# Half-size loads for the last w_out blocks, an earlier fetch of the second token tile, and new places in memory

## The chip, the cores and the metric

The kernel runs on one core of a Trainium2 chip. The metric is the device time of one execution in microseconds (us). The engines of the core are named as the profile names them: PE (TensorE; PEld is its weight load), DVE (VectorE), ACT (ScalarE), POOL (GpSimd) and SP (SyncE, which here issues nearly all transfers).

## The reference

One layer of a diffusion backbone on 2048 latent tokens of width 1024, with 256 context tokens, in fp32:

```python
hc = modulate(rmsnorm(xc, norm_mix[l]), csh1, csc1)
logf_f, k_f, logf_b, k_b, vc = hgrn2_gates(hc @ w_in[l][:, :3 * w], lb_f, lb_b, first)
hf_c = advance_state(h0, k_f, vc, jnp.cumsum(logf_f, axis=2))
hb_c = advance_state(h0, flip_t(k_b), flip_t(vc), jnp.cumsum(flip_t(logf_b), axis=2))
h = modulate(rmsnorm(x, norm_mix[l]), sh1, sc1)
o, _, _ = token_mixers(h @ w_in[l], lb_f, lb_b, first, hf_c, hb_c, *mix_args)
x = x + g1 * (o @ w_out[l])
h2 = modulate(rmsnorm(x, norm_ffn[l]), sh2, sc2)
x = x + g2 * conv_ffn(h2, w_up[l], conv_w[l], conv_b[l], w_down[l], rows)
return rmsnorm(x, norm_final)
```

`token_mixers` is a gated linear recurrence in both directions (4 heads) beside a spatial gating unit (4 heads); their outputs, 8 blocks of 128 channels, are the 8 row blocks that `w_out` (1024x1024) multiplies. `conv_ffn` is a gated MLP of width 2816 with a depthwise 3x3 convolution: up-projection, convolution and GELU, product, down-projection.

## The kernel before

Matrix products keep fp32 accuracy by splitting each operand into a high part (a copy on ACT, line 133, into the matmul's own float type) and a low part (the difference, line 134, on VectorE or GpSimd). Three matmuls stand for one product: high by high, high by low, low by high (`mm3`, line 136). All are recorded at line 65.

The work runs in four stages, one after the other on TensorE.

1. Input projection (`pj` tiles). The columns of `w_in` are taken block by block over halves of 1024 tokens, with the recurrence, the gating and preparations of later weights as generators in two queues (`hg_q`, `bg_q`), stepped between matmuls. One generator, `w_out_ops` (line 981), multiplies each 128x512 piece of `w_out` by the gate `g1`, splits it, and stores both parts to DRAM (`wo_d`).
2. Output projection (`dn` tiles out of `wo` and `o`). Sixteen token tiles of 128 rows; each takes 2 halves of 512 columns, 8 row blocks k, 3 matmuls: 48 matmuls. The operand `o` of a token tile is fetched from DRAM (`fetch_o`, line 1313) and split (`split_o`, line 1319). Tile t's operand is split before tile t-1's matmuls are written; even tiles use one buffer, odd tiles another. Between the matmuls stand the transposes and casts of the second norm (`second_norm`).
3. Up-projection (`ux`, `uz` tiles), by a 7-product scheme on 2x2 blocks, with operands `Ah`, `Al` from `a_tiles` (line 1198); the convolution runs beside it on VectorE in PSUM tiles also named `dn`.
4. Down-projection (`dn` tiles of a second pool), again 7 products, each over 11 pairs of row blocks: 77 steps n, each 8 token tiles of 3 matmuls. `prepare(n + 2)` calls `cast` (line 1541), which splits the activations into `mhl` and the weights into `thl`. After 11 steps the eight PSUM banks are emptied by `evict` (line 1789). The last product's rows are normed in `odd_sum`, `root` (line 1719) and `odd_out`.

Around the border between stages 1 and 2: during the last head, `wo_early` (line 918) loads the first three row blocks of `wo` into places that come free. Four banks before the end of stage 1, `open_wo` (line 1126) closes a pool and queues `load`, which fetches token tile 0's operand and then row blocks 3 to 7, in two column halves of 512 KB each (line 1144). The operand of tile 1 is fetched after the stage has ended, by `fetch_o(1)`.

A scheduler orders each engine's instructions by its own estimate of when they are ready. `pin` keeps an instruction behind the one written before it on its engine. Pools opened one after the other take over memory; a tile in memory that was another tile's waits for that tile's last readers.

Of the kernel before, what the change touches and what calls it, by code (L numbers as in the profile page):

```python
# [9 lines left out]
F32 = mybir.dt.float32  # L10
# [8 lines left out]
P = 128  # L19
D = 1024  # L20
# [11 lines left out]
EPS = 1e-6  # L32
LV = [1, 2, 4, 8, 16, 32, 64]
AL = 512

# [46 lines left out]
def tile_trunk(ctx, tc, x, c, cx, c_ctx, w_ada, b_ada, norm_mix, norm_ffn, w_in, hg_norm, sgu_g, sgu_b,  # L84
# [12 lines left out]
    dr = ctx.enter_context(tc.tile_pool(name="dr", bufs=1, space=DRAM))  # L97
    ident = cst.tile([P, P], F32, name="ident")
    make_identity(nc, ident)
    ones = cst.tile([P, P], F32, name="ones")  # L100
    G.memset(ones, 1.0)
    ones_r = cst.tile([P, P], F32R, name="ones_r")
    nc.gpsimd.tensor_copy(ones_r, ones)
    vec = cst.tile([P, 50], F32, name="vec")
    taps = cst.tile([P, 9 * NF], F32, name="taps")
    mhalf = cst.tile([P, 8], F32, name="mhalf")
# [24 lines left out]
    def split(hi, lo, raw, eng=None, keep=lambda i: i):  # L131

        keep(S.copy(hi, raw))  # L133
        (eng or G).tensor_sub(lo, raw, hi.bitcast(F32))  # L134
# [56 lines left out]
    with es1:  # L191
# [790 lines left out]
        def w_out_ops():  # L982

            for n in range(2):
                cl = slice(n * 512, n * 512 + 512)
                g = pm.tile([P, 512], F32, tag="acc", name="g1")
                ld(g, g_d[0:1, cl].broadcast_to([P, 512]))
                for k in range(NK):
                    raw = raw_tile().rearrange("p (a c) -> p a c", a=2)
                    hi, w = raw[:, 0, :], raw[:, 1, :]  # L990
                    ld(w, w_out[k * P:(k + 1) * P, cl])
                    yield 8.0
                    V.tensor_mul(w, w, g)
                    split(hi.bitcast(F32R), w.bitcast(F32R), w, V)
                    st(wo_d[:, k, :, cl], raw)
                    yield 1.5

        def w_down_ops():
# [128 lines left out]
        def open_wo():  # L1127
            hg_q.drain()
            gates_done()
            bg_q.drain()  # L1130
            esh.close()
            pw = esw.enter_context(tc.tile_pool(name="pw", bufs=1, side="right", reuse_waits="tile"))
            first_o.append(lambda: pw.tile([P, 2, NK, P], F32R, tag="o", name="o", align_bytes=AL))
            early = len(wo)

            def load():
                raw = raw_tile().rearrange("p (k c) -> p k c", c=P)
                ld(raw, oT_d[0][:, :, 0:P])
                for k in range(early, NK):
                    wo.append(pw.tile([P, 2, D], F32R, name=f"wo{k}", align_bytes=AL))  # L1140
                for n in range(2):
                    sl = slice(n * 512, n * 512 + 512)
                    for k in range(early, NK):
                        ld(wo[k][:, :, sl].bitcast(F32), wo_d[:, k, :, sl])
                yield 17.0
                o = first_o[0]()
                split(o[:, 0], o[:, 1], raw, V, pin)
                first_o.append(o)
                yield 0.0
            bg_q.add(load())  # L1150
# [9 lines left out]
        run_banks(seq)  # L1160
        bg_q.drain()
        hg_q.flush()

# [11 lines left out]
    xah = pb.tile([P, NR, 4, 512], F32R, tag="xah", name="xah", align_bytes=AL)  # L1177
    xal = pb.tile([P, NR - 1, 4, 512], F32R, tag="xal", name="xal", align_bytes=AL)

    turn = [0]  # L1180

    def xbank():
        return ps2.tile([P, 512], F32, tag="ux", name="ux", bufs=2)

    def zbank():
        return ps2.tile([P, 512], F32, tag="uz", name="uz", bufs=2)

    def ubank():
        turn[0] += 1
# [2 lines left out]
    def dbank():  # L1192
        return ps2.tile([P, 2, 512], F32, tag="dn", name="dn", bufs=2)

    def a_tiles():
        return tuple(px.tile([P, 4, P], F32R, tag=w, name=w, bufs=4, align_bytes=AL) for w in ("Ah", "Al"))

    def v_tile():
        return px.tile([P, TH + GW], F32, tag="cv", name="cv", bufs=3)

    def c_tile():
        return px.tile([P, NK, P], F32R, tag="fl", name="fl", bufs=2, align_bytes=AL)

    def raw_tile2(j):
        return px.tile([P, 4, 2 * P], F32, tag=f"raw{j}", name="raw")
# [2 lines left out]
    class Unit:  # L1208
# [15 lines left out]
        def prep(self, i):  # L1224

            a11, a21 = self.raw[0][:, :, :P], self.raw[0][:, :, P:]
            a12, a22 = (self.raw[1][:, :, :P], self.raw[1][:, :, P:]) if i else (None, None)
            self.A[i] = a_tiles()
            hi, lo = self.A[i]

            if i == 1:
                self.s2 = (c_tile()[:, :4, :].bitcast(F32) if self.slots[0] == 1 else
                           px.tile([P, 4, P], F32, tag="s1", name="s2"))
            split(hi, lo, (a11, a12, self.s2, a11, a21, a12, a22)[i])
            if i == 0:
                G.tensor_sub(a21, a11, a21)
            elif i == 1:
                pin(G.tensor_sub(self.s2, a22, a21))
            elif i == 2:
                G.tensor_add(a11, self.s2, a11)  # L1240
            elif i == 3:
                G.tensor_sub(a12, a12, self.s2)
# [30 lines left out]
    with tc.tile_pool(name="po", bufs=1, reuse_waits="tile") as po:  # L1273
        def second_norm(hh, g0, xs, ss, bank_, first, step):

            r = rstd(px, ss, 2, 1.0 / D)
            for i in range(2):
                scaled.append(V.tensor_scalar(out=xs[i], in0=xs[i], scalar1=r[:, i:i + 1], scalar2=None, op0=ALU.mult))
            yield first
            cl = slice(g0 // 2 * P, g0 // 2 * P + P)  # L1280
            for k in range(4):
                pt = bank_()
                for kk in range(2):
                    for i in range(2):
                        o = kk * 256 + i * P
                        T.transpose(pt[:, o:o + P], xs[i][:, (k + 4 * kk) * P:(k + 4 * kk + 1) * P], ident)
                yf = c_tile()
                fl = yf.bitcast(F32)
                for kk, dims in ((0, [[7 * P, 2], [1, P]]), (1, [[4 * P, 2], [1, P]])):
                    kq = k + 4 * kk  # L1290
                    pin(S.activation(view(fl, kk * P, dims),
                                     pt[:, kk * 256:kk * 256 + 256].rearrange("p (i c) -> p i c", c=P),
                                     AF.Identity, bias=s2[:, kq:kq + 1], scale=a2[:, kq:kq + 1]))
                pin(V.tensor_sub(fl[:, 3:5, :], view(fl, 7 * P, [[-2 * P, 2], [1, P]]), view(fl, 0, [[7 * P, 2], [1, P]])))
                V.tensor_sub(fl[:, 2, :], fl[:, 5, :], fl[:, 3, :])
                V.tensor_sub(fl[:, 6, :], fl[:, 1, :], fl[:, 2, :])
                hi = px.tile([P, 7, P], F32R, tag="yst", name="yst", bufs=2, align_bytes=AL)
                a = b = 0
                if hh == 0:
                    a, b = NR, NR - 1  # L1300
                    S.copy(xah[:, :, k, cl], fl[:, :a, :])
                    V.tensor_sub(xal[:, :, k, cl], fl[:, :b, :], xah[:, :b, k, cl].bitcast(F32))
                    V.tensor_sub(yf[:, b:a, :], fl[:, b:a, :], xah[:, b:a, k, cl].bitcast(F32))
                split(hi[:, a:, :], yf[:, a:7, :], fl[:, a:7, :], V)
                st(yd[hh][:, 0, a:, k, cl], hi[:, a:, :].bitcast(F32))
                st(yd[hh][:, 1, b:, k, cl], fl[:, b:7, :])
                yield step
# [9 lines left out]
            return raw  # L1317

        def split_o(t, raw):
            o = po.tile([P, 2, NK, P], F32R, tag="o", name="o", align_bytes=AL) if t % 2 else first_o[0]()  # L1320
            split(o[:, 0], o[:, 1], raw, V, pin)
            return o

# [2 lines left out]
            ld(xt.rearrange("p a b -> p (a b)"), x[t * P:(t + 1) * P, :])  # L1326
            return xt.rearrange("p a b -> p (a b)")

        raw_o = {1: fetch_o(1)}
        xts = {0: fetch_x(0)}  # L1330
        ops = {0: first_o[1]}
        xs = []
        for t, (hh, g) in enumerate(tiles):
            if g % 2 == 0:
# [205 lines left out]

    def cast(n, a, b, at, bt):

        split(*at, a, V)
        split(*bt, b, V)
        ops[n] = *at, *bt

    def down(pd, n, i, first, last):
# [18 lines left out]
    for n, (u, i) in enumerate(prods):  # L1566
# [18 lines left out]
        if n == 11:  # L1585
            bg_q.drain()
        if n == 12:
            edges = px.tile([P, 7, P], F32R, tag="yst", name="edges", bufs=2, align_bytes=AL).bitcast(F32)
            edges = edges[:, :4, :].rearrange("p f (w c) -> p f w c", w=2)
        with tc.issue_after(scaled[-1].ins) if n < 8 else nullcontext():  # L1590
            after(u, i, p)
# [37 lines left out]
    pd_ = ctx.enter_context(tc.tile_pool(name="pd", bufs=1, reuse_waits="tile"))  # L1629
    sT = pb.tile([P, NR * 4 * 512], F32, tag="xah", name="sT", align_bytes=AL)  # L1630
    sS = pd_.tile([P, NJ, TH], F32, tag="sS", name="sS", align_bytes=AL)
    thl = pd_.tile([P, 3, 2, 512], F32R, name="thl", align_bytes=AL)
    odd = [pd_.tile([P, 2, 512], F32, name=f"odd{i}") for i in range(NCH)]
    even = [pd_.tile([P, 2, 512], F32, name=f"even{i}") for i in range(NCH)]
    nf = pd_.tile([P, D], F32, name="nf")
    nw = [0]
# [82 lines left out]
    def root(ss, plus=D * EPS):  # L1719

        a, r = (pd_.tile([P, 1], F32, tag=t, name=t, bufs=4) for t in ("ra", "rr"))
        G.tensor_scalar(out=a, in0=ss, scalar1=plus, scalar2=None, op0=ALU.add)  # L1722
        G.tensor_tensor(out=r, in0=a, in1=mhalf[:, :1], op=ALU.pow)  # L1723
        return r

# [63 lines left out]
    def evict(q, i, pd):  # L1789
        o, e = odd[i], even[i]  # L1790
        if q in (0, 2):
            S.copy(o[:, q // 2, :], pd)
        elif q in (1, 5):
            V.tensor_add(e[:, q // 5, :], pd, e[:, q // 5, :])
        elif q in (3, 4):
            V.tensor_add(o[:, 0, :], pd, o[:, 0, :])
        sums_behind(q, i)
# [65 lines left out]
```

## Time and profile before

| What | Value |
|---|---|
| Time of three runs, median (lowest to highest) | 2437.95 us (2434.5 to 2441.58) |
| The profiled execution's own time | 2440.39 us |
| Its span (first to last instruction) | 2438.6 us |
| TensorE busy | 2402.0 us (99%) |
| VectorE, ScalarE, GpSimd busy | 1656.9, 1043.2, 867.8 us |
| Mean granted TensorE clock | 0.996 |
| Moved by DMA | 396.43 MB, mean 163 GB/s |

A busy share is an average over stages. Matmuls are pipelined, so the mean duration of one (389 ns) is longer than the step from one start to the next. An idle time in brackets stands before the instruction on its line, with the one that ended it.

### The profile page before, as it was taken

The numbers are of one execution on the slowest core, as the hardware profiler recorded it, in microseconds if no ns is written. First come the engines' busy times: TensorE is split into PE (matmuls) and PEld (weight loads), VectorE is DVE, ScalarE is ACT, GpSimd is POOL, SyncE is SP. The second block draws the span as 40 slices with busy tenths as digits, with TensorE's granted clock in tenths as the row PEclk, the third lists the DMA queues.
The fourth block names the chain that finished last, engine by engine and source line by source line (L and its number), as shares of the span: only waits on it lengthen the run. The fifth ranks groups of instructions, "written<-read, shape, count | busy, mean of one in ns | idle before, by whom it ended". The sixth has DMA issues, their size and how long they took to land.

```text
span 2438.6 us, 32286 instructions
## 1 busy us (share of the span) xinstructions
PE 2402.0 (99%) x11711; PEld 1995.0 (82%) x11711; DVE 1656.9 (68%) x2253; ACT 1043.2 (43%) x1802; POOL 867.8 (36%) x788
## 2 busy tenths in 40 slices
PE   8999999999999999999999999999999999999998
PEld 5887887888888888788888888888888887888887
DVE  5757795765786785465596666639866772776875
ACT  3654344444444443354554444434445442332343
POOL 0021110210121122000688778787888870000002
PEclk9999999999999999999999999999999999999999
DMA  8365445463355234668922322562222238934755
GB/s 302 117 206 169 148 143 168 153 234 111 114 195 173 88 103 160 223 208 264 303 80 90 96 81 91 179 235 97 86 94 85 88 112 336 324 121 147 229 152 198
DMA packets 305581, 396.43 MB, mean 163 GB/s; under 512 B 32633, under 2 KB 215681, under 8 KB 302349
## 3 DMA queue, kind: packets, MB, share of 16 engines
q1 hardware_dynamic: 302132, 393.61, 48.6%
q8 instruction: 92, 1.51, 0.3%
q10 hardware_dynamic: 3289, 0.76, 0.1%
q14 instruction: 68, 0.56, 0.1%
HBM read 285.18 MB, written 109.13 MB: 162 GB/s over the span
## 4 chain that ended last, share of the span: by engine, by line
PE 54%; issue 2%; DMA 1%; DVE 1%; POOL 1%; ACT 1%; SPq 0%; POOLq 0%; ACTq 0%; DVEq 0%
PE dn L65 20%; PE ux L65 19%; PE uz L65 14%; PE pj L65 0%; POOL ra L1722 0%; DMA raw<-in_x_dram 0%; POOL rr L1723 0%; PE ux L69 0%; DMA raw<-in_w_up_dram 0%; DMA yf<-yd 0%; PE uz L69 0%; DVE dn L1433 0%; DMA yd<-fl 0%; POOL Al L134 0%; DVE cv L1357 0%
## 5 line engine op out<-in xcount | busy, mean ns | idle before, releaser
L1433 DVE SCALAR_TENSOR_TENSOR dn<-gp,taps,dn 128x1024 f32<-128x1024 f32 x352 | 448.2, 1284 | 97.5 <-ACT dn L1430 93.1
L65 PE MATMUL dn<-thl,mhl 128*128 128x512 f32 x1680 | 381.5, 389 | 1.2 <-ACT thl L133 1.2
L65 PEld LDWEIGHTS dn<-thl,mhl 128*128 128x128 f32 x1680 | 315.0, 188 | 67.7 <-ACT thl L133 2.1
L134 POOL TENSOR_TENSOR Al<-raw,Ah 128x512 fp32r<-128x512 f32 x264 | 341.7, 1311 | 65.8 <-ACT Ah L133 41.5
L65 PE MATMUL pj<-xh,whi 128*128 128x512 f32 x896 | 362.3, 405 | 0.3 <-ACT whi L133 0.3
L65 PE MATMUL pj<-xh,wlo 128*128 128x512 f32 x896 | 351.1, 392 | 1.2 <-DVE wlo L134 1.2
L65 PE MATMUL pj<-xl,whi 128*128 128x512 f32 x896 | 351.7, 393 | 0.0
L133 ACT CAST Ah<-raw 128x512 fp32r<-128x512 f32 x264 | 162.9, 620 | 238.9 <-PE ux L65 133.1
L65 PE MATMUL ux<-xah,Ah 128*128 128x512 f32 x528 | 205.7, 390 | 0.3 <-ACT keep L1497 0.3
L65 PEld LDWEIGHTS pj<-xh,wlo 128*128 128x128 f32 x896 | 168.3, 188 | 37.5 <-DVE wlo L134 2.1
L65 PEld LDWEIGHTS pj<-xh,whi 128*128 128x128 f32 x896 | 168.7, 188 | 34.2 <-issue 3.5
L65 PEld LDWEIGHTS pj<-xl,whi 128*128 128x128 f32 x896 | 168.9, 189 | 30.0 <-DVE xl L253 0.2
L65 PE MATMUL dn<-wo,o 128*128 128x512 f32 x768 | 184.4, 396 | 2.6 <-ACT o L133 2.1
L65 PE MATMUL uz<-yf,Ah 128*128 128x512 f32 x704 | 174.0, 389 | 0.0
L65 PEld LDWEIGHTS dn<-wo,o 128*128 128x128 f32 x768 | 143.0, 189 | 32.8 <-ACT o L133 2.5
L591 POOL TENSOR_TENSOR K<-K,tot 128x512 f32<-128x512 f32 x40 | 62.9, 1572 | 299.9 <-DVE tot L521 154.6
L65 PE MATMUL ux<-yf,Ah 128*128 128x512 f32 x528 | 155.4, 389 | 0.0
L65 PEld LDWEIGHTS uz<-yf,Ah 128*128 128x128 f32 x704 | 132.1, 188 | 27.4
L65 PE MATMUL ux<-xah,Al 128*128 128x512 f32 x528 | 141.8, 390 | 1.0 <-POOL Al L134 0.9
L65 PE MATMUL ux<-xal,Ah 128*128 128x512 f32 x352 | 137.0, 389 | 0.0
L1722 POOL TENSOR_SCALAR ra<-ss 128x1 f32<-128x1 f32 x8 | 5.3, 662 | 360.4 <-ACT jk L1714 360.4
L134 DVE TENSOR_TENSOR wlo<-raw,whi 128x1024 fp32r<-128x1024 f32 x68 | 84.1, 1236 | 68.3 <-ACT whi L133 67.3
(341 smaller groups left out, 4452.7 us busy)
## 6 DMA issues: line engine op xcount, KB each, us to landing
raw<-in_w_up_dram SPq DMA_DIRECT2D x88, 512.0 KB, 3.6
mr<-m SPq DMA_DIRECT2D x85, 512.0 KB, 5.5
raw<-in_w_in_dram SPq DMA_DIRECT2D x68, 512.0 KB, 4.0
sT<-wd SPq DMA_DIRECT2D x88, 256.0 KB, 5.8
raw<-in_w_ada_dram SPq DMA_DIRECT2D x32, 512.0 KB, 4.6
yf<-yd SPq DMA_DIRECT2D x14, 1024.0 KB, 10.4
m<-cv SPq DMA_DIRECT2D x22, 544.0 KB, 2.7
raw<-in_w_down_dram SPq DMA_DIRECT2D x22, 512.0 KB, 4.0
```

The lines of the kernel that those rows point to most:

```text
L65: return self.engine.matmul(out, lhsT, rhs, **kw)
L133: keep(S.copy(hi, raw))
L134: (eng or G).tensor_sub(lo, raw, hi.bitcast(F32))
L591: e.tensor_mul(view(K2, row * W + o, src), view(K, o, src), view(tot, t0, [[4, n], [ts, 2], [0, B]]))
L1433: V.scalar_tensor_tensor(out=cr, in0=gt[:, t // 3:t // 3 + RH, t % 3:t % 3 + GW], scalar=taps[:, t * NF + f:t * NF + f + 1], in1=cr, op0=A ...
L1722: G.tensor_scalar(out=a, in0=ss, scalar1=plus, scalar2=None, op0=ALU.add)
```

## The change

It has these parts:

- Row blocks k = 5, 6, 7 of `w_out` (`LATE`) are no longer split in stage 1: the product with the gate alone is stored, and at the border only that is loaded (256 KB for a half instead of 512 KB) and split there, behind the last bank of stage 1, on ACT and VectorE, the low part in the loaded data's place.
- The operand of token tile 1 is fetched into a tile of its own, `raw1`, directly behind the row blocks, instead of by `fetch_o(1)` after the stage.
- In stage 4, `thl` is placed behind the first five `odd` tiles; the copies of `cast` (steps 3 to 65) and of `evict` are pinned in the written order on ACT.
- `root` adds a tensor where it added a scalar operand read from memory.
- Places: `ones` shares the memory of `ones_r`; the late `wo` tiles share one tag; `Ah` and `Al` share one tag of eight buffers; some tiles no longer ask for a multiple of 512 bytes, and `s2` is made 80 elements longer; the PSUM tags of stages 2 and 3 are laid out in a fixed order, `uz` as two tags of one buffer each.

```diff
+LATE = (5, 6, 7)
...
-    ones = cst.tile([P, P], F32, name="ones")
-    G.memset(ones, 1.0)
     ones_r = cst.tile([P, P], F32R, name="ones_r")
-    nc.gpsimd.tensor_copy(ones_r, ones)
+    nc.gpsimd.tensor_scalar(out=ones_r, in0=ident, scalar1=0.0, scalar2=1.0, op0=ALU.mult, op1=ALU.add)
+    ones = ones_r.bitcast(F32)
...
                     V.tensor_mul(w, w, g)
-                    split(hi.bitcast(F32R), w.bitcast(F32R), w, V)
-                    st(wo_d[:, k, :, cl], raw)
+                    if k in LATE:
+                        st(wo_d[:, k, 0, cl], w)
+                    else:
+                        split(hi.bitcast(F32R), w.bitcast(F32R), w, V)
+                        st(wo_d[:, k, :, cl], raw)
...
                 for k in range(early, NK):
-                    wo.append(pw.tile([P, 2, D], F32R, name=f"wo{k}", align_bytes=AL))
+                    wo.append(pw.tile([P, 2, D], F32R, tag="wo", name="wo", bufs=NK - early, align_bytes=AL))
                 for n in range(2):
                     sl = slice(n * 512, n * 512 + 512)
                     for k in range(early, NK):
-                        ld(wo[k][:, :, sl].bitcast(F32), wo_d[:, k, :, sl])
+                        if k in LATE:
+                            ld(wo[k][:, 1, sl].bitcast(F32), wo_d[:, k, 0, sl])
+                        else:
+                            ld(wo[k][:, :, sl].bitcast(F32), wo_d[:, k, :, sl])
+                raw1 = pw.tile([P, NK, P], F32, name="raw1")
+                ld(raw1, oT_d[0][:, :, P:2 * P])
+                first_o.append(raw1)
                 yield 17.0
...
         bg_q.drain()
         hg_q.flush()
+        for n in range(2):
+            sl = slice(n * 512, n * 512 + 512)
+            for k in LATE:
+                t = wo[k][:, :, sl]
+                split(t[:, 0], t[:, 1], t[:, 1].bitcast(F32), V, pin)
...
     def zbank():
-        return ps2.tile([P, 512], F32, tag="uz", name="uz", bufs=2)
+        turn[1] += 1
+        return ps2.tile([P, 512], F32, tag=f"uz{turn[1] % 2}", name="uz")
...
+    for first in (xbank, zbank, dbank, zbank):
+        first()
...
-        return tuple(px.tile([P, 4, P], F32R, tag=w, name=w, bufs=4, align_bytes=AL) for w in ("Ah", "Al"))
+        return tuple(px.tile([P, 4, P], F32R, tag="A", name=w, bufs=8, align_bytes=AL) for w in ("Ah", "Al"))
...
-            o = po.tile([P, 2, NK, P], F32R, tag="o", name="o", align_bytes=AL) if t % 2 else first_o[0]()
+            o = po.tile([P, 2, NK, P], F32R, tag="o", name="o") if t % 2 else first_o[0]()
...
-        raw_o = {1: fetch_o(1)}
+        raw_o = {1: first_o[1]}
...
-        split(*at, a, V)
-        split(*bt, b, V)
+        keep = pin if 3 <= n < 6 * NJ else lambda i: i
+        split(*at, a, V, keep)
+        split(*bt, b, V, keep)
...
+    odd = [pd_.tile([P, 2, 512], F32, name=f"odd{i}") for i in range(5)]
     thl = pd_.tile([P, 3, 2, 512], F32R, name="thl", align_bytes=AL)
-    odd = [pd_.tile([P, 2, 512], F32, name=f"odd{i}") for i in range(NCH)]
+    odd += [pd_.tile([P, 2, 512], F32, name=f"odd{i}") for i in range(5, NCH)]
...
-        G.tensor_scalar(out=a, in0=ss, scalar1=plus, scalar2=None, op0=ALU.add)
+        if isinstance(plus, float):
+            G.tensor_scalar(out=a, in0=ss, scalar1=plus, scalar2=None, op0=ALU.add)
+        else:
+            G.tensor_add(a, ss, plus)
...
         if q in (0, 2):
-            S.copy(o[:, q // 2, :], pd)
+            pin(S.copy(o[:, q // 2, :], pd))
```

More of the change, by code (lines that the diff above doesn't have):

```diff
@@ L1201, in c_tile @@
     def c_tile():
-        return px.tile([P, NK, P], F32R, tag="fl", name="fl", bufs=2, align_bytes=AL)
+        return px.tile([P, NK, P], F32R, tag="fl", name="fl", bufs=2)
     def raw_tile2(j):
@@ L1232, in prep @@
                 self.s2 = (c_tile()[:, :4, :].bitcast(F32) if self.slots[0] == 1 else
[L1233 removed]
+                           px.tile([P, 4 * P + 80], F32, tag="s1", name="s2")[:, :4 * P].rearrange("p (k c) -> p k c", k=4))
             split(hi, lo, (a11, a12, self.s2, a11, a21, a12, a22)[i])
@@ L1296, in second_norm @@
                 V.tensor_sub(fl[:, 6, :], fl[:, 1, :], fl[:, 2, :])
-                hi = px.tile([P, 7, P], F32R, tag="yst", name="yst", bufs=2, align_bytes=AL)
+                hi = px.tile([P, 7, P], F32R, tag="yst", name="yst", bufs=2)
                 a = b = 0
@@ L1587, in tile_trunk @@
         if n == 12:
-            edges = px.tile([P, 7, P], F32R, tag="yst", name="edges", bufs=2, align_bytes=AL).bitcast(F32)
+            edges = px.tile([P, 7, P], F32R, tag="yst", name="edges", bufs=2).bitcast(F32)
             edges = edges[:, :4, :].rearrange("p f (w c) -> p f w c", w=2)
```

4 lines of the change are left out of this document (2 added, 2 removed).

## The prediction

> **What bounds the kernel now.** I read the head of the page first, then TensorE's waits, then the order of time around each wait. The page says which engine sets the end:
>
> ```profile
> span 2438.6 us, 32286 instructions
> PE 2402.0 (99%) x11711; PEld 1995.0 (82%) x11711; DVE 1656.9 (68%) x2253; ACT 1043.2 (43%) x1802; POOL 867.8 (36%) x788
> 1237.76 5.44 PE ux L65 x24
> ```
>
> TensorE is busy in all but 37 us of the span. The third line, from the chain of work that ended last, gives its pace: 24 matmuls of 128x512 in 5.44 us, 0.2267 us from start to start. The change removes no matmul, so only stalls, clock and the ends of the program can give anything. TensorE's waits (engine and line, waited for whom: us, times, longest) name the candidates:
>
> ```profile
> PE pj L65 <- DMA wa<-in_w_ada_dram: 3.3, 4, 1.5
> PE sc L65 <- DVE kl L800: 2.7, 2, 2.0
> PE dn L65 <- ACT o L133: 2.1, 1, 2.1
> PE dn L65 <- ACT thl L133: 1.2, 2, 0.8
> PE dn L65 <- DVE o L134: 0.5, 1, 0.5
> ```
>
> The third and fifth are the border between the input projection and the output projection, the fourth is the down stage; the change works on both. The first two lie in the projection, where it only takes side work away.
>
> **The border.** The order of time there (start, duration, engine, line; in brackets the idle time before and who ended it):
>
> ```profile
> 962.94 0.39 SPq L1144 DMA_DIRECT2D wo<-wo_d  x1
> 963.72 0.59 SPq L1138 DMA_DIRECT2D raw<-oT  x1
> 964.35 7.24 SPq L1144 DMA_DIRECT2D wo<-wo_d  x9
> 969.95 1.05 ACT L133 CAST o<-raw 128x1024 fp32r<-128x1024 f32 x1 [2.81 <-DMA raw<-oT]
> 972.96 0.60 ACT L690 ACTIVATE gu<-pj 128x512 f32<-128x512 f32 x1 [1.96 <-PE pj L65]
> 973.43 2.95 SPq L686 DMA_DIRECT2D oT<-nt  x2
> 973.57 11.15 PE L65 MATMUL dn<-wo,o 128*128 128x512 f32 x48
> 973.85 0.75 DVE L717 SCALAR_TENSOR_TENSOR nt<-mi,vec,rh 128x512 f32<-128x512 f32 x1 [1.59 <-PE mi L65]
> 976.48 0.83 SPq L1316 DMA_DIRECT2D raw<-oT  x1
> 977.35 3.17 SPq L1326 DMA_DIRECT2D raw<-in_x_dram  x1
> 985.70 1.04 ACT L133 CAST o<-raw 128x1024 fp32r<-128x1024 f32 x1 [12.15 <-DMA raw<-in_x_dram]
> 986.78 1.22 DVE L134 TENSOR_TENSOR o<-raw,o 128x1024 fp32r<-128x1024 f32 x1 [12.18 <-ACT o L133]
> 986.80 0.73 PE L65 MATMUL dn<-wo,o 128*128 128x512 f32 x2 [2.08 <-ACT o L133]
> 988.06 18.24 PE L65 MATMUL dn<-wo,o 128*128 128x512 f32 x73 [0.52 <-DVE o L134]
> ```
>
> Token tile 0 takes 48 matmuls from 973.57. Tile 1 should follow at 984.56 (the last of the 48 starts 0.39 us, one matmul, before 984.72; plus one pace), but its operand is fetched only at 976.48, behind ten row-block loads and two stores, and is cast at 985.70. TensorE starts at 986.80 and stops again for the low part until 988.06. Late by the second restart: 988.06 - (984.56 + 2 x 0.2267) = 3.05 us. After it, 73 matmuls take 18.24 us; at the pace they need 72 x 0.2267 + 0.39 = 16.71, so another 1.53 us goes. The clock tells why (PE busy, other engines, granted clock, DMA share, GB/s in each stretch):
>
> ```profile
> 411.00:415.60 4.60, 2.67 (x11) 1.69 (x9) 2.86 (x4) 2.16 (x3) 0.00 (x0) 1.00 0.58 171
> 415.60:419.10 3.50, 3.44 (x15) 2.84 (x16) 3.47 (x4) 1.07 (x2) 0.00 (x0) 1.00 0.07 26
> 984.50:988.00 3.50, 0.95 (x3) 0.30 (x2) 1.22 (x2) 1.04 (x1) 0.00 (x0) 0.95 0.80 255
> 988.00:991.10 3.10, 3.04 (x7) 2.46 (x8) 1.14 (x2) 1.87 (x3) 0.00 (x0) 0.51 0.43 119
> 973.50:984.50 11.00, 11.00 (x51) 8.98 (x50) 0.75 (x1) 0.06 (x1) 1.29 (x1) 1.00 1.07 394
> ```
>
> For 3.1 us behind this stall the clock is at 0.51, which is half of 3.1, about 1.5 us. The 2.0 us stall near 415 us is followed by a full clock. The border therefore costs 3.05 + 1.53 = 4.6 us. [...]
>
> What the change does to it. Six of the ten loads (k = 5, 6, 7, both halves) halve from 512 to 256 KB, 1.57 MB less, 4.0 us at the 394 GB/s of the last row. The fetch of tile 1 goes behind them and ahead of the two stores, instead of behind both: 0.52 MB, 1.3 us. The loads need
>
> ```profile
> wo<-wo_d SPq DMA_DIRECT2D x10, 512.0 KB, 10.6
> ```
>
> 10.6 us from issue to landing. The last of ten, issued by 971.6 (964.35 + 7.24), lands near 982.2 now; the fetch behind them will land near 982.2 - 4.0 + 1.3 = 979.5, its cast ends at 980.5, its low part (1.22) at 981.8: 2.8 us before 984.56. Far end: the odd tile's memory may still be held by the last `nt` store, issued at 976.1 now; with the 8.4 us that the old fetch took from 977.3 to 985.7 that is 984.5, less 4.0 - 1.3 = 2.7 makes 981.8, and the cast and low part end at 984.1. Both ends clear 984.56. I take the whole 4.6, with 2.6 left over as the low end, should one wait of 2 us remain without the slow clock.
>
> What it adds. Six splits: a 128x512 copy on ACT and a subtraction on VectorE each, now behind the last projection bank. Their durations stand in the down stage:
>
> ```profile
> 2027.08 0.62 ACT L133 CAST thl<-sT 128x512 fp32r<-128x512 f32 x1 [8.19 <-PE dn L65]
> 2027.73 0.69 DVE L80 TENSOR_TENSOR thl<-sT,thl 128x512 fp32r<-128x512 f32 x1 [7.58 <-DMA sT<-wd]
> ```
>
> They are pinned on ACT behind `gu`, free at 973.56; VectorE has one `nt` until 974.60. Within tile 0 block 5 is wanted after 15 matmuls, at 976.97, block 6 at 977.65, block 7 at 978.33 (low parts one pace later); the second half from 982.4. If the data is there, copies end at 974.2, 974.8, 975.4 and low parts by 976.7: no wait. Is it? The three loads are issued at about 965.2 to 966.8 (second to fourth of the nine in 7.24 us, 0.8 us each). The operand fetch of 963.72 was in use at 969.95, 6.2 us later, the median is 10.6: block 7 lands between 973.0 and 977.4, and at the late end its low part is ready at 978.7 against 978.56, block 5's at 977.1 against 977.20. Cost 0 to 0.5 us; I take 0, since the row of the neighbouring issue is the nearer one. What queues behind a late load: ACT's next copies, then the cast of tile 1, which has the margin above. Taken away from the projection are six copies and six subtractions (1.3 us each pair) beside TensorE: nothing on the path.
>
> **The down stage.**
>
> ```profile
> 2026.61 0.39 PE L65 MATMUL dn<-Ah,mhl 128*128 128x512 f32 x1
> 2027.75 2.61 PE L65 MATMUL dn<-thl,mhl 128*128 128x512 f32 x10 [0.75 <-ACT thl L133]
> 2013.25 0.81 SPq L1651 DMA_DIRECT2D sT<-wd  x1
> 2065.78 5.83 PE L65 MATMUL dn<-thl,mhl 128*128 128x512 f32 x25
> 2068.02 2.54 ACT L1792 COPY odd<-dn 128x512 f32<-128x512 f32 x5 [11.35 <-PE dn L65]
> 2071.36 0.66 ACT L133 CAST thl<-sT 128x512 fp32r<-128x512 f32 x1
> 2072.07 4.17 PE L65 MATMUL dn<-thl,mhl 128*128 128x512 f32 x17 [0.46 <-ACT thl L133]
> ```
>
> The first cast into `thl` waited 8.19 us for TensorE: its place lies over the `Ah`/`Al` pairs that products 0 to 2 read to the end, while its `sT` had been issued at 2013.25. Five `odd` tiles (first written at 2068) now take that place. The next matmul was due at 2026.61 + 0.23 = 2026.84 and came at 2027.75: 0.91 us back. Next in line there is product 4, 5.4 us later, with both copies ready. At 2068 the scheduler put five evictions, which wait for TensorE, ahead of the casts, with ACT idle for 11.35 us before; with casts and evictions pinned in written order, the cast comes first. Due: last start 2065.78 + 5.83 - 0.39 = 2071.22, plus 0.23; came at 2072.07: 0.62 us back. The evictions then start up to 1.7 us later (1.05 + 0.62), which no one waits for: the next use of the first bank is at 2071.5.
>
> **The rest.** At the very end `root` gets a tensor addition for a scalar operand read from memory:
>
> ```profile
> L1722 POOL TENSOR_SCALAR ra<-oss 128x1 f32<-128x1 f32 x8 | 3.8, 477 | 40.8 <-ACT dn L1748 40.8
> L1448 POOL TENSOR_TENSOR cv<-edges 128x64 f32<-128x64 f32 x22 | 7.2, 326 | 3.2 <-issue 3.2
> L1517 POOL TENSOR_TENSOR cv<-keep,cv 128x512 f32<-128x512 f32 x44 | 56.9, 1293 | 3.2 <-DVE keep L1516 2.4 <-ACT cv L1447 0.7
> ```
>
> No row shows a 128x1 addition. The two others grow by 967 ns over 448 elements, so one element costs about 326 - 63 x 2.16 = 190 ns: 0.3 us less on the last link, between 0.15 (the 64-wide price) and 0.45. The bank order, the two `uz` tags, the common tag for `Ah`/`Al`, `ones` and the dropped alignment requests change no instruction's size and no order of use: 0, at worst 0.1 us where tile 0's first bank is one that `gu` reads until 973.56.
>
> **Sum.** 4.6 + 0.9 + 0.6 + 0.3 = 6.4 us. The profiled execution's own time is 2440.39 us (span 2438.6): it would become 2434.0. It lies 2.4 us above the median of the runs, 2437.95 (2434.5 to 2441.58), so against the median I forecast 2431.5 us.
>
> **Rivals.** (1) The stall shrinks but stays: tile 1 or the late blocks come 2 us late. For it: the queue runs full here. Against it: the margins above. Gain 4.6 - 2.0 + 1.8 = 4.4, or 2.9 if the slow clock stays too: about 2434.3. (2) The projection is reordered for the better: the stall of 2.0 us at 415.65 stands behind VectorE's step for the k = 5 block of `w_out`, which loses its split. Then 2.2 us more: 2429.3. Against it: the multiplication that waits for the load remains. (3) Slower: the six splits wait for the whole backlog. If ACT's first copy gets its data only when the last load of today does, at up to 985.7, block 5 is ready at 987.0, TensorE stops for 10 us from 976.97 and runs 3.1 us at half clock: 11.5 lost, 6.4 gained, 2443. It turns negative from a landing at about 980.6, 15 us after issue, against 10.6 in the row. (4) The stall at tile 1 has another cause, such as memory held by a store that lands no earlier: only 1.8 us is gained, 2436.2.
>
> **Chances.** Forecast 0.58, (1) 0.15, (2) 0.12, (3) 0.07, (4) 0.08. A measurement of this kernel tells about 0.3%, 7.3 us, from no change. The forecast lies just inside; with the runs' spread of 3.5 us either way, 0.4 of its chance (0.23) and three quarters of (2) (0.09) fall beyond, and 0.03 for gains that I have not priced: faster 0.35. Slower by over 0.3% needs (3) with a second stall, or a pace lost somewhere: 0.06. Within is the rest, 0.59. The range reaches from (2) with the spread to (1) and (4) with it: 2425 to 2440.
>
> **What would show it.** Right: no wait of `dn` on `o` in TensorE's waits, a granted clock of 1.00 through 970 to 1000, tile 1's cast before tile 0's last matmul, no wait on `thl`, `ra` near 0.2 us. Wrong: a wait of `dn` on `wo`, a clock near 0.5 between 975 and 995, new idle time in the projection, or a pace other than 0.227 us in matmuls of the odd tiles' operand, whose alignment is no longer asked for.

## The result and the profile after

The changed kernel takes 2432.98 us in the median of 19 runs (2430.53 to 2435.98), the kernel before 2437.55 in 19 runs beside it (2434.37 to 2441.75). The ratio is 0.9982, with a 95% interval of 0.9975 to 0.9989: 4.4 us less (2.7 to 6.1). The profiled execution of the changed kernel has an own time of 2434.03 us, 6.36 less than that of before.

From the page after, the span, the busy times, and the row of the down stage's matmuls (the last column is TensorE's idle time before them):

```profile
span 2432.2 us, 32291 instructions
PE 2400.6 (99%) x11711; PEld 1994.5 (82%) x11711; DVE 1658.0 (68%) x2253; ACT 1044.1 (43%) x1802; POOL 865.0 (36%) x787
L66 PE MATMUL dn<-thl,mhl 128*128 128x512 f32 x1680 | 381.0, 389 | 0.0
```

The span fell by 6.4 us and TensorE's busy time by 1.4. TensorE's waits after no longer have a row for `dn`; at their head are waits of the input projection, of the start of the program and of the up-projection:

```profile
PE sc L66 <- DVE K L591: 2.4, 4, 0.9
PE pj L66 <- POOL ident masks.py:199: 2.2, 1, 2.2
PE ux L66 <- POOL Al L134: 1.6, 3, 0.6
PE sc L66 <- DVE kl L800: 1.1, 2, 0.8
```

One of these the change made longer. The wait on `ident` at the start was 1.5 us before; with `ones_r` now made out of `ident`, the first matmul starts at 2.23 or 2.24 us in all ten profiles with this part, and at 1.45 in the four without it. It costs nothing later: 33 us on, behind waits for loads of `wa`, the last matmul on `wa` starts at 34.84 to 35.77 us in the ten and at 34.87 to 35.30 in the four.

The order of time at the border after:

```profile
963.80 1.64 SPq L1148 DMA_DIRECT2D wo<-wo_d  x3
966.68 2.95 SPq L1148 DMA_DIRECT2D wo<-wo_d  x3
969.98 0.57 SPq L1152 DMA_DIRECT2D raw<-oT  x1
971.68 0.60 ACT L690 ACTIVATE gu<-pj 128x512 f32<-128x512 f32 x1 [2.83 <-PE pj L66]
972.10 3.32 SPq L686 DMA_DIRECT2D oT<-nt  x2
972.17 1.65 ACT L133 CAST wo<-wo 128x512 fp32r<-128x512 f32 x3
972.29 17.95 PE L66 MATMUL dn<-wo,o 128*128 128x512 f32 x78
973.24 4.19 DVE L134 TENSOR_TENSOR wo<-wo 128x512 fp32r<-128x512 f32 x5
974.52 1.23 ACT L133 CAST wo<-wo 128x512 fp32r<-128x512 f32 x2 [0.70 <-DMA wo<-wo_d]
977.06 0.62 ACT L133 CAST wo<-wo 128x512 fp32r<-128x512 f32 x1 [1.31 <-DMA wo<-wo_d]
980.09 1.05 ACT L133 CAST o<-raw 128x1024 fp32r<-128x1024 f32 x1 [2.42 <-DMA raw<-in_x_dram]
981.18 1.23 DVE L134 TENSOR_TENSOR o<-raw,o 128x1024 fp32r<-128x1024 f32 x1 [2.77 <-ACT o L133]
```

TensorE goes through tile 0 and into tile 1 without a stop (78 matmuls in 17.95 us: 77 steps of 0.228 and one of 0.39). The six copies stand behind `gu`, the first three with no wait for their loads. Tile 1's cast begins 7.80 us after tile 0's first matmul, against 12.13 before. The clock stays full where it was 0.51 (the stretches have TensorE's busy time, the other engines', the granted clock, DMA share and GB/s):

```profile
971.00:985.00 14.00, 14.00 (x67) 11.73 (x66) 8.00 (x9) 5.30 (x9) 2.69 (x2) 1.00 0.99 338
985.00:988.00 3.00, 3.00 (x15) 2.49 (x14) 1.15 (x1) 1.82 (x3) 0.00 (x0) 1.00 0.82 266
988.00:991.00 3.00, 3.00 (x15) 2.45 (x15) 0.08 (x1) 0.00 (x0) 0.00 (x0) 1.00 0.66 217
```

In the down stage after, the first product with `thl` follows its predecessor at the pace (2022.24 to 2022.47), and the casts come ahead of the evictions:

```profile
2022.24 0.39 PE L66 MATMUL dn<-Ah,mhl 128*128 128x512 f32 x1
2022.47 1.75 PE L66 MATMUL dn<-thl,mhl 128*128 128x512 f32 x7
2061.48 0.61 ACT L133 CAST thl<-sT 128x512 fp32r<-128x512 f32 x1
2062.62 4.16 ACT L1815 COPY odd<-dn 128x512 f32<-128x512 f32 x8 [0.53 <-PE dn L66]
```

I compare the two profiles by stages, each measured from one first matmul to the next in the order of time, so that what a stage does to later ones is not counted twice:

| Stage | Before, us | After, us | Difference |
|---|---|---|---|
| Start to tile 0's first matmul | 973.57 | 972.29 | -1.28 |
| Border: tile 0's first matmul to the first transpose of the second norm | 32.57 | 27.99 | -4.58 |
| From there to the last rows of the up-projection | 1000.99 | 1002.52 | +1.53 |
| From there to the down stage's tail (its last product's last rows) | 402.41 | 400.50 | -1.91 |
| Tail to the end | 29.03 | 28.92 | -0.11 |
| Span | 2438.57 | 2432.22 | -6.35 |

The border and the down stage carry the change. The first and the third row move by over a microsecond too, with opposite signs; whether these two belong to the change was a question for the runs.

### The profile page after: what moved, and what is told of

Read it like the earlier page. It is cut to its first block, busy times and chain, and to the rows that moved or that the text cites. A ratio compares the mean times of both kernels' runs of the same rounds, so it can differ in the third digit from the quotient of the medians.

```text
span 2432.2 us, 32291 instructions
## 1 busy us (share of the span) xinstructions
PE 2400.6 (99%) x11711; PEld 1994.5 (82%) x11711; DVE 1658.0 (68%) x2253; ACT 1044.1 (43%) x1802; POOL 865.0 (36%) x787
## 4 chain that ended last, share of the span: by engine, by line
PE 49%; issue 2%; POOL 1%; DMA 1%; DVE 0%; ACT 0%; SPq 0%; POOLq 0%; ACTq 0%; DVEq 0%
PE ux L66 19%; PE dn L66 16%; PE uz L66 14%; DMA raw<-in_w_up_dram 1%; POOL rr L1746 0%; DMA yf<-yd 0%; POOL Al L134 0%; DMA xn<-cv 0%; POOL ra L1745 0%; POOL ra L1743 0%; DVE fl L134 0%; PE ux L70 0%; ACT jk L1734 0%; ACT yst L133 0%; POOL raw L1260 0%
```

## The experiments

**Which half of the border change does the work.** Three kernels were timed, with the changed kernel again beside them.

No late row blocks, and the second token tile fetched behind the stage; the other parts of the change are kept, and the lines of the early fetch are taken out:

```diff
-LATE = (5, 6, 7)
+LATE = ()
...
-        raw_o = {1: first_o[1]}
+        raw_o = {1: fetch_o(1)}
```

> The changed kernel with both border edits undone: LATE is empty, so row blocks 3 to 7 are split in stage 1 and loaded whole, and tile 1's operand is fetched after the stage. All else as changed. My theory (the border edits take the wait of tile 1's operand, worth 4.6 us in one profile): this one keeps dn waiting on o for about 2.6 us and a granted clock near 0.5 behind it, and stands 1.8 us under the kernel before. Rival (the new places in memory do it): no such wait here, and about 6 us under the kernel before.

Only the early fetch (the first edit without the second):

> The changed kernel with LATE empty: the early fetch alone, ten whole loads ahead of it. My theory (the queue's length sets the time): the fetch lands 4.0 us later than in the changed kernel, near 983.5 on the scale of before; the high part is in time, the low part about 1 us late; the clock stays at 1.00; 1 us over the changed kernel. Rival (the odd tile's memory is held by the last nt store, which now stands behind one more load): the cast comes near 985 to 986, the wait is 1.5 us or more again, and the slow clock may come back: 2.5 to 4.6 us over the changed kernel.

Only the late row blocks, with the fetch behind the stage (the second edit, without the first):

> The changed kernel with tile 1's operand fetched after the stage as before: half-size loads alone. My theory: the old fetch now lands 4.0 us earlier, at about 981.5 on the scale of before, the low part is ready by 983.8, no wait of dn on o, and the time is the changed kernel's within 0.5 us: the early fetch would be a margin and not a gain. Rival (its place in the queue behind the two stores sets it): still a wait of 1 us or more at tile 1, 2 us or more over the changed kernel.

The changed kernel once more:

> The changed kernel once more, for a second profile: its one profile was 6.4 us under the one profile of before, its median 4.6 us. If the missing 1.8 us is in the start of the up-projection (1.1 us of new idle time there, behind a w_up load), that idle time is here too and ux/uz wait 1.5 us or more between 1170 and 1225. If it is that before is slowed by the half clock only in some executions, the idle time here may be anything, and executions of before differ by about 1.5 us at the border.

Measured beside the kernel before:

| Kernel | Runs | Median, us | Mean, us | Ratio to before (95%) |
|---|---|---|---|---|
| before | 33 | 2438.55 | 2438.8 | |
| neither | 11 | 2435.97 | 2437.1 | 0.9996 (0.9987 to 1.0004) |
| early fetch alone | 11 | 2438.14 | 2437.5 | 0.9992 (0.9983 to 1.0002) |
| late blocks alone | 11 | 2433.99 | 2434.4 | 0.9981 (0.9972 to 0.9990) |
| changed, again | 11 | 2434.82 | 2435.1 | 0.9987 (0.9979 to 0.9996) |

The median with neither stands lower than its ratio says, since its runs spread over 7.6 us. In the mean the late blocks alone stand 2.7 us under it (1.2 to 4.3 when the runs are drawn again at random). So the late blocks alone reach what the whole change reaches, and the fetch adds nothing that can be measured, with them or without. For the early fetch alone the rival came nearer than the theory: both parts are late, by stops of 0.90 and 0.53 us, at a full clock, and the median is 3.3 us over the changed kernel's. The order of time with the early fetch alone:

```profile
973.55 0.59 SPq L1152 DMA_DIRECT2D raw<-oT  x1
974.75 11.15 PE L66 MATMUL dn<-wo,o 128*128 128x512 f32 x48
974.81 5.04 SPq L686 DMA_DIRECT2D oT<-nt  x2
985.71 1.04 ACT L133 CAST o<-raw 128x1024 fp32r<-128x1024 f32 x1 [10.97 <-DMA raw<-in_x_dram]
986.80 0.74 PE L66 MATMUL dn<-wo,o 128*128 128x512 f32 x2 [0.90 <-ACT o L133]
988.07 4.15 PE L66 MATMUL dn<-wo,o 128*128 128x512 f32 x17 [0.53 <-DVE o L134]
```

The fetch is issued ahead of the two stores, and the cast still begins only 10.96 us behind tile 0's start. The name in the bracket is not the cause: by the trace's records of semaphores the fetch had landed at 984.24, and the cast followed 0.18 us after the landing of the last `nt` store, 985.53. The trace also has the waits of ACT itself ahead of this cast: the one on the first store's semaphore was over at 984.98, the one on the semaphores of the second store and of the fetch at 985.55, 0.02 us after the second store's landing. So the cast does wait for the store, as it must if that store reads memory that the odd tile takes over. In the changed kernel the same store landed at 979.92, 0.17 us ahead of the cast, and the fetch at 978.65. With the late blocks alone it is the fetch that lands last (979.37, cast 979.55). An earlier fetch thus helps only down to the landing of that store, and makes the store itself no earlier: it landed 10.78 us behind tile 0's start here, and 9.37 to 10.36 us in the five profiles with whole loads and the fetch behind it. In these runs only fewer bytes in the queue brought both forward.

**The store off the queue.** Built on the kernel with the early fetch alone, the last head's last two `nt` stores were issued by ACT:

```diff
-                    st(oT_d[hh][:, 4 + h, n0:n0 + 512], zt)
+                    (S.dma_start if (hh, h) == (1, NH - 1) else st)(oT_d[hh][:, 4 + h, n0:n0 + 512], zt)
```

> The early fetch alone (whole loads, LATE empty) with the stores of the last head's gating tiles issued on ACT instead of SP. In the early fetch alone, tile 1's cast came at 985.71, although the semaphore records have its fetch landing at 984.24 and the last of these stores at 985.53. Theory (the odd tile's memory is held by that store): the store lands earlier here and the cast follows the fetch, so the idle time at tile 1 falls from 1.43 us to under 0.6. Rival (the fetch's own landing sets it): the idle time stays within 0.4 us of 1.43.

```profile
971.32 0.37 ACTq L686 DMA_DIRECT2D oT<-nt  x1
971.78 1.04 ACT L133 CAST o<-raw 128x1024 fp32r<-128x1024 f32 x1 [5.84 <-POOL nt L685]
972.88 0.73 PE L66 MATMUL dn<-wo,o 128*128 128x512 f32 x2 [0.26 <-ACT o L133]
974.14 10.76 PE L66 MATMUL dn<-wo,o 128*128 128x512 f32 x46 [0.53 <-DVE o L134]
977.18 0.57 SPq L1152 DMA_DIRECT2D raw<-oT  x1
984.74 1.04 ACT L133 CAST o<-raw 128x1024 fp32r<-128x1024 f32 x1 [11.42 <-DMA raw<-in_x_dram]
985.84 0.73 PE L66 MATMUL dn<-wo,o 128*128 128x512 f32 x2 [0.94 <-ACT o L133]
987.16 5.05 PE L66 MATMUL dn<-wo,o 128*128 128x512 f32 x21 [0.58 <-DVE o L134]
```

The stop did not shrink: 0.94 and 0.58 us at tile 1, as the rival has it. One run took 2437.04 us. Two things went against the forecast. ACT waited 5.84 us for the product that the first store sends, so tile 0's own cast came late (0.26 and 0.53 us of stop at its start). And the fetch was issued 3.63 us later than in the kernel without this edit, and its own landing (984.49) became the last thing ahead of the cast. The edit itself did that: the first store, now on ACT, uses the semaphore of the fetch, and SyncE waited on it until 977.12, 0.02 us after that store's landing. This run therefore shows that this way of taking the stores off does not pay with full loads; it does not test cleanly whether the store alone held the cast in the run before, for which the landings and ACT's own waits are the evidence.

**How many bytes are enough.** One and two late blocks instead of three, with the fetch behind the stage:

```diff
-LATE = (5, 6, 7)
+LATE = (7,)
```

> The changed kernel with one late row block (k = 7) in place of three, and the second token tile fetched behind the last bank as before. Measured so far: with no late block TensorE stopped for 2.23 us ahead of tile 1, with three not at all. Theory (the bytes ahead of the last store decide): one block less is 0.52 MB, 1.3 us at 394 GB/s, so the stop before tile 1's high part shrinks to about 0.9 us (0.5 to 1.3), the one before its low part stays near 0.5, and the clock stays at 1.00; from tile 0's first matmul to the first transpose of the up-projection 29.4 us (28.9 to 29.9) against 32.31 with none and 27.99 with three. Rival (only the splits' place or the issue order matters, not the bytes): 27.99 or over 30.

> The changed kernel with two late row blocks (k = 6, 7), the second token tile fetched behind the last bank as before. Theory (bytes): 1.05 MB less than with none, 2.7 us against a stop of 2.23: tile 1's cast comes in time by 0.4 us, at most the wait for its low part is left, 0 to 0.4 us; tile 0 to first transpose 28.0 to 28.4 us, clock 1.00. Rival (only three blocks, or the fetch ahead of the stores, are enough): over 29 us.

In the order of time with one late block, one stop is left, for the low part:

```profile
972.73 11.93 PE L66 MATMUL dn<-wo,o 128*128 128x512 f32 x50
982.83 1.05 ACT L133 CAST o<-raw 128x1024 fp32r<-128x1024 f32 x1 [2.60 <-DMA raw<-in_x_dram]
985.19 5.06 PE L66 MATMUL dn<-wo,o 128*128 128x512 f32 x21 [0.53 <-DVE o L134]
```

In that with two there is none:

```profile
972.87 19.31 PE L66 MATMUL dn<-wo,o 128*128 128x512 f32 x84
981.36 1.05 ACT L133 CAST o<-raw 128x1024 fp32r<-128x1024 f32 x1 [2.38 <-DMA raw<-oT]
```

From these and the other profiles, with times counted from tile 0's first matmul (by an estimate from tile 1's due time of 10.99 us and the 1.05 and 1.23 us of its cast and subtraction, the cast must begin by about 9.9 us for the high part and 9.1 for the low part to be in time; stops under 0.15 us are left out):

| Kernel | Late blocks | Cast of tile 1 begins, us | Stops, us | Slow clock | Border, us |
|---|---|---|---|---|---|
| before | 0 | 12.13 | 2.08, 0.52 | yes | 32.57 |
| before, again | 0 | 11.40 | 1.35, 0.52 | no | 30.46 |
| neither | 0 | 12.28 | 2.23 | yes | 32.31 |
| early fetch alone | 0 | 10.96 | 0.90, 0.53 | no | 30.00 |
| one late block | 1 | 10.10 | 0.53 | no | 29.15 |
| two late blocks | 2 | 8.49 | none | no | 28.00 |
| late blocks alone | 3 | 8.40 | none | no | 27.99 |
| changed | 3 | 7.80 | none | no | 27.99 |

The border with one late block was forecast at 29.4 us and came at 29.15, with two at 28.0 to 28.4 and came at 28.00. But the stop ahead of the high part with one block was forecast at 0.5 to 1.3 us and is 0.04. Bytes at 394 GB/s, 1.3 us a block, explain the direction and not the sizes: the first block brings the cast 1.3 to 2.2 us forward (from 11.40 or from 12.28, which is how far single profiles differ), the second 1.6, the third 0.1. The fetch behind the stage took 9.20 us from issue to landing with no late block, 7.02 with one, 5.09 with two and 5.00 with three. What holds it at 5 us was not tried. The third block is not needed for the time, and neither is the fetch; the fetch is margin.

**The two parts of the down stage, each put alone into the kernel before.** The place of `thl` behind five `odd` tiles:

```diff
+    odd = [pd_.tile([P, 2, 512], F32, name=f"odd{i}") for i in range(5)]
     thl = pd_.tile([P, 3, 2, 512], F32R, name="thl", align_bytes=AL)
-    odd = [pd_.tile([P, 2, 512], F32, name=f"odd{i}") for i in range(NCH)]
+    odd += [pd_.tile([P, 2, 512], F32, name=f"odd{i}") for i in range(5, NCH)]
```

> The kernel before with one edit: thl is placed behind five of the odd tiles. My theory: the wait of 0.75 us in front of product 3 goes, 0.9 us from step to step, and the wait of 0.46 us at the first change of banks stays (the evictions still stand ahead of the cast on ACT). Rival (the two waits are one, the later one handed down): both go.

The pins of casts and evictions alone (the edits in `cast` and `evict` of the diff above):

> The kernel before with one edit: the copies of cast and evict are pinned in the written order on ACT. My theory: the wait at 2072 goes, 0.6 us from step to step, and the wait in front of product 3 stays at 0.75 us. Rival (an early cast pinned behind another one that waits for its buffer): a new wait in the first products of the down stage, 1 us or more.

The kernel before, beside both:

> The kernel before once more, for a second profile. If the stall at tile 1 and the half clock behind it are there in each execution, the border costs 4.6 us again (first matmul of the output projection to the first transpose 32.6 us; 28.0 in the changed kernel). If the half clock comes only when the stall falls well in some free-running window, the stall stands and the clock stays at 1.00: about 31 us. For the second half of the output projection and the start of the up-projection (fifth group of transposes to the last up-projection product: 905.35 us in the one profile of before, 906.85 and 907.04 in two of the changed kernel): 906.5 or more here means jitter, 905.5 or less means that the change costs over a microsecond there.

The border of the kernel before, again, is 30.46 us at a full clock, near the 31 us of the second of its forecasts: the half clock comes in some executions only. From the fifth group of transposes on it has 905.81 us, between the two marks that were set for it.

One run each took 2438.24, 2434.01 and 2436.15 us, too few to order them; the parts are read in the stage. TensorE's waits of `dn` with the place alone:

```profile
PE dn L65 <- ACT o L133: 2.1, 1, 2.1
PE dn L65 <- ACT thl L133: 0.5, 1, 0.5
```

The same waits with the pins alone:

```profile
PE dn L65 <- ACT o L133: 1.3, 1, 1.3
PE dn L65 <- ACT thl L133: 0.8, 1, 0.8
PE dn L65 <- DVE o L134: 0.5, 1, 0.5
```

Each edit removes one of the two waits on `thl` and leaves the other. From the first down matmul to the first with `thl`: 17.67 us before, 17.67 with the pins, 16.72 with the place, 16.72 in the changed kernel. From there to the tail: 381.79 before, 381.66 with the place, 381.00 with the pins, 380.83 in the changed kernel. From the last rows of the up-projection to the tail, the place is worth 1.08 us, the pins 0.79, both together 1.91.

**The tail.** The changed kernel with the former operation of `root`:

```diff
-        if isinstance(plus, float):
-            G.tensor_scalar(out=a, in0=ss, scalar1=plus, scalar2=None, op0=ALU.add)
-        else:
-            G.tensor_add(a, ss, plus)
+        G.tensor_scalar(out=a, in0=ss, scalar1=plus, scalar2=None, op0=ALU.add)
```

> The changed kernel with the former operation of root, a scalar operand read from memory. Forecast before: 0.3 us longer from the last matmul to the end. By the two profiles: 0.11 us longer (7.50 against 7.38), since the addition of 128x1 takes 0.41 us beside VectorE's work and 0.50 with the scalar. Rival (the 0.11 has another source): 7.38 as in the changed kernel.

It took 2431.96 us in one run, and 7.51 us from the last matmul's start to the end, against 7.38 in the changed kernel and 7.50 before. The forecast by the two profiles, 0.11 us, holds (0.13). The addition in the changed kernel, by its line (duration in ns: shortest, median, longest):

```profile
L1745 POOL TENSOR_TENSOR ra<-oss x8: 193/414/416, 2407.7 to 2426.8; 128x1 f32<-128x1 f32 x8
```

**A version with later steps for `w_out`.** The generator rests for 11 us in place of 8 between the issue of a piece's loads and the multiplication:

```diff
-                    yield 8.0
+                    yield 11.0
```

> The changed kernel, with the generator of w_out's pieces resting for 11 us in place of 8 between the issue of a piece's loads and the multiplication by the gate. Theory: the stop of TensorE near 413 us (2.0 us in the profile of before, 0.3 to 2.1 in others) comes from VectorE waiting there for that load; 3 us later it has landed, so no stop over 0.5 us there and 0 to 1.5 us less than the changed kernel in the median: ratio to before 0.9976 to 0.9984. Rival (the stop is not the load's, or another one takes its place): the changed kernel's 0.998 to 0.999, with a stop elsewhere between 400 and 700 us.

2432.3 us against 2439.49 of before: 0.9970 (0.9959 to 0.9981). Of this version's waits in the projection two rows matter:

```profile
PE sc L66 <- ACT knh L821: 1.4, 1, 1.4
PE sc L66 <- DVE kl L800: 0.7, 1, 0.7
```

The wait on `kl` near 412 us is 0.74 us, over the 0.5 that was forecast and between the 0.33 and 1.15 of two profiles of the changed kernel. One of 1.4 us on `knh` came at 795.60, where the other profiles have none over 0.1. Its ratio lies under the range forecast for it, 0.9976 to 0.9984, so neither theory nor rival has it. Its interval overlaps those of the changed kernel (0.9975 to 0.9989, 0.9979 to 0.9996), so that it is faster than the changed kernel was not shown.

## Why the prediction was right, and where a size was off

The forecast was 2431.5 us in a range of 2425 to 2440; the measured median is 2432.98. By its steps:

- **Border, 4.6 us forecast: right for the profiled pair (4.58), too much for the median.** The profile of before happened to show one of the long borders. Five profiles with full loads and the fetch behind the stage have borders of 32.57, 30.46, 32.24, 30.38 and 32.31 us (before, before again, `thl` alone, pins alone, neither), 31.6 in the mean, against 27.99: the change is worth 3.6 us there on the average, 2.4 where the clock stays full, and 4.3 to 4.6 where it halves. The step that was mis-sized is "I take the whole 4.6", which set the long stop and the slow clock of one execution for every execution.
- **When tile 1 is ready.** The forecast took the cast's end at 980.5 and the low part's at 981.8, that is 6.9 and 8.2 us behind tile 0's start; they came at 8.9 and 10.1. The far end of that estimate, the odd tile's memory held by the last store, 10.5 us, was the mechanism that held (that store lands last in all four profiles with both parts), and 11.4 would still have been in time for the low part. This is the memory that rival (4) speaks of; its gain was not lost, because the store landed earlier too (7.63 us behind tile 0's start, 10.23 before). By the forecast's own measure the margin was 0.9 us (10.99 - 10.12), not 2.8, and the smaller loads make it. The fetch, which the forecast put on an equal footing, adds a little margin (the cast begins at 7.2 to 8.3 us in four profiles with both parts, at 8.4 without the fetch) and no time.
- **The six splits, 0 us: right.** The first three copies ran at -0.1 to 1.5 us from tile 0's start (forecast 0 to 1.8), and TensorE waited for no `wo`. Rival (3), the splits behind the whole backlog, did not happen: the last late piece was copied at 977.06.
- **Down stage, 0.91 + 0.62 = 1.53: 1.08 and 0.79 alone, 1.91 together.** Both gaps were right: matched matmul by matmul, the ones behind the two waits come 0.91 and 0.62 us sooner. The sum left out the next step. The second matmul behind each wait started 0.34 us after the first (2027.75 to 2028.09, and 2072.07 to 2072.41) in place of 0.23, so each wait cost 0.11 us more; the remaining 0.06 to 0.16 us was not traced to single matmuls.
- **Tail, 0.3: 0.1.** The step that was mis-sized is the price of the 128x1 addition. The 190 ns were there in the first of the eight, 193, but the other seven, the last link among them, take 0.41 us, against 0.50 for the operation before. The sign "`ra` near 0.2 us" did not come.
- **Rival (2), the projection reordered for the better: not settled.** The stop at the k = 5 block was 1.99 us before and 0.33 after, as that rival has it. In both, VectorE waits there for a load of `w_out` (1.74 and 0.73 us), and the stop differs from execution to execution: 0.68 to 2.11 us in the nine profiles in which the k = 5 block is still split in stage 1 (with one and with two late blocks, 1.89 and 1.90, it still is), 0.33 to 1.17 in the four in which it is not, the later steps left aside. The means are 1.58 and 0.80, so up to 0.8 us may be the change's; the ranges overlap. Tile 0's start, 969.03 to 974.75 us in the nine and 971.15 to 972.29 in the four, does not tell them apart, so the -1.28 of the first table row cannot be put down to the change.
- **Not foreseen: the +1.53 us in the third row.** From the fifth group of transposes to the last rows of the up-projection, the five profiles with full loads and the fetch behind the stage have 905.35 to 906.39 us, the seven with late blocks 905.35 to 907.04; this begins in the middle of the output projection. The means differ by 0.4 us. Four profiles with every part of the change in this stage have 905.55, 905.64, 906.85 and 907.04 us, so the scatter of one and the same code is larger than the difference. With it go TensorE's waits for `Al` in the up-projection, 1.6 us in the two profiles of the changed kernel, 0.9 and 1.0 in the other two of these four, 0.9 and 1.1 in the two of before; a loss of about 0.4 us may be there, and it stays open.

The sum of the mean terms is 3.6 + 1.9 + 0.1 = 5.6 us, against a measured 4.4 (2.7 to 6.1); the forecast's 6.4 us lies above that interval. The forecast's own-time figure, 2434.0 against 2434.03, is closer than its terms deserve, and that is luck: -1.28 and +1.53 nearly cancel, and 0.4 us too little in the down stage stands against 0.2 too much in the tail.

## What to carry to other kernels

Where a transfer is late behind a full queue, ask first how many bytes stand ahead of it, and what its destination's memory still waits for: here, moving the transfer forward helped only as far as the store that freed the memory, and halving bytes brought both forward. Count a slow-clock stretch from one profile as a term that some executions pay and others don't, and take the range from several profiles. A tile placed over memory with late readers, and casts queued behind evictions, show up as short waits on one stage's first use; each was worth 0.8 to 1.1 us here, and the edits were a few lines.

## What the hardware showed

The half clock does not follow from the length of a stop alone. In two profiles the same matmul waits 1.89 and 1.90 us for the same operand. With one late block, in the order of time:

```profile
411.88 0.50 PE L66 MATMUL sc<-kl,ones_r 128*128 128x512 f32 x1 [1.89 <-DVE kl L800]
```

The stretch that holds the stop, and the next (TensorE's busy time is the second number, the clock the third from the end):

```profile
409.59:413.00 3.41, 1.52 (x6) 1.03 (x7) 3.01 (x4) 1.31 (x3) 0.00 (x0) 1.00 0.43 127
413.00:416.41 3.41, 3.41 (x10) 2.63 (x9) 3.38 (x4) 1.80 (x4) 0.00 (x0) 0.50 0.39 150
```

With two late blocks, in the order of time:

```profile
414.81 0.50 PE L66 MATMUL sc<-kl,ones_r 128*128 128x512 f32 x1 [1.90 <-DVE kl L800]
```

And its stretches:

```profile
411.16:414.57 3.41, 1.75 (x7) 0.94 (x5) 1.76 (x3) 2.16 (x3) 0.00 (x0) 1.00 0.77 231
414.57:417.98 3.41, 3.17 (x14) 2.60 (x15) 3.41 (x5) 1.07 (x2) 0.00 (x0) 1.00 0.00 0
```

The stretches are not chosen freely. In the clock records of each of the fourteen profiles, every change of clock while the program runs lies 3.413 us, or a whole multiple of it, from the others, so each execution has a grid of such stretches. With one late block the whole stop falls into one stretch, TensorE is idle for 1.89 us of it, and the next runs at 0.50. With two, an edge of the grid (414.57) cuts the stop, the first stretch has 1.66 us idle, and the clock stays at 1.00.

The border between the stages goes the same way. Stops of 2.08, 2.14 and 2.23 us put 2.17, 2.09 and 2.17 us of idle time into one stretch (before, `thl` alone, neither), and a half clock of 3.41 us followed each; the kernel before, again, has 1.65 us in one and the early fetch alone 1.43, and none followed. From 60 to 2425 us these four stretches are the only ones with a half clock behind them, and no other has more than 1.66 us idle. By these traces, then, what decided was how much of a stop fell into one stretch, with the limit somewhere between 1.66 and 1.89 us; no run varied it on purpose. It is not the whole rule: in the first 60 us, stretches with 1.0 to 1.6 us idle were followed by a half clock too. The Trainium skill, "TensorE: Matmul & The Clock Gate", section "HAM oscillation", gives the rule that TensorE should have no idle gaps over about 3.4 us. As a limit for keeping the full clock these traces do not bear that rule out, since stops of 1.89 to 2.23 us were followed by the half clock.
